# Layer 1's input projection by seven products of quarters instead of eight, with the sums of weights made by accumulating DMAs

## The chip, the cores and the metric

The kernel runs on one core of one Trainium2 chip. TensorE multiplies matrices, VectorE (DVE), ScalarE (ACT) and GpSimd (POOL) work on tiles of 128 partitions, and 16 DMA engines move data between HBM and SBUF; they are fed by the queues of SP, ScalarE and GpSimd, each of which issues in order. The metric is the time of one execution on the device in microseconds, the median of several runs.

## The reference

Two layers over 1024 tokens of 2048 channels. Layer 0 is an attention layer. Layer 1, to which the change belongs, is a pooling layer:

```python
h = _rmsnorm(x, pre_g) * (1 + scale) + shift            # 1024 x 2048
proj = h @ w_in                                         # w_in: 2048 x 4096
y = _multiscale_pool(proj[..., :POOL_WIDTH], pool_w, pool_scale) * jax.nn.silu(proj[..., POOL_WIDTH:])
x = x + gate * _rmsnorm(y @ w_out, post_g)
```

`_multiscale_pool` takes four groups of 512 channels, subtracts each value from the mean over 2, 4, 8 or 16 positions, and multiplies each group by a 512 x 512 matrix. The first 2048 columns of `w_in` give the values u, the other 2048 the gates.

## The kernel before

Everything is in float32. A product is made in three passes on TensorE (`PASSES`): each operand is split into a rounded part h and a rest l (`split`: ScalarE casts, VectorE subtracts), and hh, hl and lh are summed in PSUM. One pass of one k (128 rows) on one tile of 128 columns and 512 tokens is one matmul of 128x512.

Weights come by `w_tiles`: a raw tile `wr` of 512 KB (four k x 256 columns, two buffers) is loaded on SP's queue and split into tiles `wh` and `wl` of two k each (four buffers each). Before, one such pair serves two column tiles, two k and both halves of the tokens, 24 products.

The order of the stages is that of the code, and a scheduler settles the order on each engine when the kernel is built; what is pinned (`keep_in_program_order`) stays. The attention runs over 32 units (a group of four heads and 128 queries). In each, GpSimd multiplies the gate tile `zt` by the inverse sums `rs` (L857), which SP has sent through memory (`lsd`, `rs`), and VectorE multiplies the unit's output by it (`y`, L863); only then is the PSUM bank of the output free for the next unit. Then the output projection runs for the first half of the tokens (n = 0) and for the second (n = 1); its result is transposed (L1053), scaled and split into the operand tiles `hT`, 16 k for each half. While the last rows of n = 1 are normalised, `first_gates` computes the first six gate tiles of n = 0 (L1034, stored in `sd`). Layer 1's projection follows by groups: `project1` for four value tiles of both halves, `pooled` (the window sums, alternating between VectorE and GpSimd, L1097), `project1` for the gates, and the pooled products `mx`. The results `yt` (one buffer) are stored to `y1d` for the last output projection.

Of the kernel before, what the change touches and what calls it, by code (L numbers as in the profile page):

```python
# [17 lines left out]
P = 128  # L18
# [17 lines left out]
LEAD = 28  # L36
LAG = 2
# [8 lines left out]
BRIDGE = 6  # L46
# [30 lines left out]
def tile_backbone(ctx, tc, ins, out):  # L77
# [13 lines left out]
    def dram(shape, name):  # L91
        return tc.dram_tile(shape, F32, name=name)
# [46 lines left out]
    sd = [dram([P, HL], f"sd{m}") for m in range(BRIDGE)]  # L139
    y1d = [[dram([P, 4, 2, HL], f"y1d{g}_{n}") for n in range(NH)] for g in range(4)]  # L140

# [646 lines left out]
    with ExitStack() as st:  # L788
# [41 lines left out]
        GATE = nc.gpsimd  # L830

# [73 lines left out]
        for u, (g, n) in enumerate(units):  # L905
# [7 lines left out]
            for c in order(u):  # L913
# [5 lines left out]
                elif c == "P":  # L919
                    product()  # L920
                elif c == "N":
                    nxt = start(u + 2)
                    next(nxt, None)
                else:
                    weights = next(ahead, None) or weights
            if u in SUMS:
                mod_sums(SUMS.index(u))
# [14 lines left out]
    def out_proj(ev, w, y, gps, n, resid, finish, ahead=None, last=False):  # L942
# [15 lines left out]
        def gated(t, cg, ps, gp):  # L958
            o = ev.tile([P, 512], F32, tag="og", name="og", bufs=18)
# [48 lines left out]
    hT = [[None] * NH for _ in range(KC)]  # L1008
    with ExitStack() as st:
# [16 lines left out]
        def first_gates():  # L1026

            for m0 in range(0, BRIDGE, 2):
                outs = [psg.tile([P, HL], F32, tag="g", name="g") for _ in range(2)]
                for k0, nk, w in w_tiles(ins["od_w_in"][0][:, (16 + m0) * P : (18 + m0) * P], 2 * P):  # L1030
                    for m, o in enumerate(outs):
                        for k in range(k0, k0 + nk):
                            for i, (a, b) in enumerate(PASSES):
                                mm = nc.tensor.matmul(  # L1034
                                    o, lhsT=w[a][:, k - k0, m * P : (m + 1) * P], rhs=hT[k][0][:, b],
                                    start=(k == 0 and i == 0), stop=(k == KC - 1 and i == 2),
                                )
                                tc.keep_in_program_order(mm)
                        yield
                for m, g in enumerate(outs, m0):  # L1040
                    zt = ev.tile([P, HL], F32, tag="og", name="zt", bufs=18)
                    nc.scalar.activation(zt, g, AF.Silu)
                    store(sd[m], zt)

        for n in range(NH):
            og = out_proj(ev, ins["ev_w_out"][0], ys[n], gpd[0], n, lambda t: x[t * P : (t + 1) * P, :], add_norm, None if n else other_half(yd))
            gates = first_gates() if n else iter(())
            list(islice(gates, LEAD))
            for k in range(KC):
                list(islice(gates, 1))  # L1050
                t = pst.tile([P, HL], F32, tag="t", name="t")
                for tb in range(4):
                    tr = nc.tensor.transpose(t[:, tb * P : (tb + 1) * P], og[tb][k // 4][:, (k % 4) * P : (k % 4 + 1) * P], ident)  # L1053
                    if n:
                        tc.keep_in_program_order(tr)
                w = ev.tile([P, HL], F32, tag="nw", name="nw", bufs=2)
                nc.scalar.activation(w, t, AF.Identity, bias=b1[:, k : k + 1], scale=s1[:, k : k + 1])
                hT[k][n] = act_tile(k, n)
                split(hT[k][n][:, 0], hT[k][n][:, 1], w, "pool")
            list(gates)  # L1060


    w_in1 = ins["od_w_in"][0]
    with ExitStack() as st:
        ev = pool(st, "ev2")
# [104 lines left out]
```

## Time and profile before

| | |
|---|---|
| median of 3 runs | 3043.45 us (3042.88 to 3043.84) |
| the profiled execution | 3042.5 us, its span 3040.8 us |
| granted TensorE clock, mean | 0.989 |
| TensorE busy | 2951.6 us, 97% |
| VectorE, ScalarE, GpSimd busy | 1612.4, 1067.0, 169.3 us |
| DMA moved | 530.32 MB, mean 174 GB/s |

The span runs from the first to the last instruction; the rest of the execution's time lies around it. A share of 97% is a mean over stages; what a change in one stage is worth is read in its own windows.

### The profile page before, as it was taken

What the parts mean: (1) busy time and instruction counts of PE and PEld (TensorE: products, weight loads), DVE (VectorE), ACT (ScalarE), POOL (GpSimd) and SP (SyncE); (2) the same over time, 40 slices, a digit from 0 to 9 for tenths busy, and PEclk for the clock granted to TensorE, in tenths of its full rate; (3) what the DMA queues carried; (4) which work ended last, traced back from release to release, by engine and by line L of the source; (5) the groups of instructions that cost most, each with busy time, mean ns of one, the idle gap of its engine ahead of it and who ended that gap; (6) DMA issues with size and microseconds to landing.
All of it is one profiled execution on the core that took longest, in us unless ns stands there. A gap on an engine that the chain in (4) does not pass through costs nothing.

```text
span 3040.8 us, 38187 instructions
## 1 busy us (share of the span) xinstructions
PE 2951.6 (97%) x14038; PEld 2456.4 (81%) x14038; DVE 1612.4 (53%) x2866; ACT 1067.0 (35%) x2060; POOL 169.3 (6%) x150
## 2 busy tenths in 40 slices
PE   5999999999999999999899999999999999999998
PEld 4788888778887878888778888888888888888887
DVE  7979875663347478888633543533333323233434
ACT  5553322211212267766632443522222212122322
POOL 0000000000000000002200210300000002000000
PEclk8999999999999999999999999999999999999999
DMA  8858878886668554446554635414122121454634
GB/s 314 291 179 258 257 238 260 280 291 218 210 220 298 178 151 142 115 150 167 143 188 157 237 97 170 150 49 143 45 95 76 63 90 49 151 191 146 252 109 163
DMA packets 373009, 530.32 MB, mean 174 GB/s; under 512 B 28644, under 2 KB 215894, under 8 KB 371670
## 3 DMA queue, kind: packets, MB, share of 16 engines
q1 hardware_dynamic: 287990, 445.81, 45.5%
q10 hardware_dynamic: 84832, 82.07, 7.9%
q8 instruction: 110, 1.80, 0.2%
q14 instruction: 77, 0.63, 0.1%
HBM read 428.88 MB, written 98.91 MB: 174 GB/s over the span
## 4 chain that ended last, share of the span: by engine, by line
PE 80%; DMA 11%; DVE 5%; issue 2%; ACT 1%; POOL 0%; SPq 0%; ACTq 0%; DVEq 0%; POOLq 0%
PE g L184 41%; PE g L953 21%; DMA mraw<-in_od_mod_w_dram 5%; PE o L895 4%; PE mx L184 3%; PE s L252 3%; PE t L841 3%; DVE mac L345 2%; PE g L1034 2%; DMA mraw<-in_ev_mod_w_dram 2%; DMA lsd<-ls 1%; DMA rs<-lsd 1%; DMA wr<-in_od_w_out_dram 1%; PE c L258 1%; DMA zt<-in_ctx_dram 1%
## 5 line engine op out<-in xcount | busy, mean ns | idle before, releaser
L147 DVE TENSOR_TENSOR wl<-wr,wh 128x512 fp32r<-128x512 f32 (+1 forms) x576 | 395.8, 692 | 843.2 <-ACT wh L144 831.1
L144 ACT CAST wh<-wr 128x512 fp32r<-128x512 f32 (+1 forms) x576 | 350.5, 616 | 1152.3 <-PE g L184 584.3
L184 PE MATMUL g<-h,wh 128*128 128x512 f32 x2368 | 743.0, 394 | 1.9 <-ACT h L144 1.8
L953 PE MATMUL g<-wh,a 128*128 128x512 f32 x1920 | 593.7, 390 | 0.4 <-ACT wh L144 0.4
L184 PE MATMUL g<-a,wh 128*128 128x512 f32 x1856 | 571.2, 389 | 0.0
L184 PEld LDWEIGHTS g<-h,wh 128*128 128x128 f32 x2368 | 445.3, 190 | 93.6 <-ACT h L144 2.5
L184 PE MATMUL g<-h,wl 128*128 128x512 f32 x1184 | 465.0, 393 | 5.0 <-DVE wl L147 5.0
L953 PEld LDWEIGHTS g<-wh,a 128*128 128x128 f32 x1920 | 360.2, 188 | 75.1 <-ACT wh L144 0.8
L345 DVE SCALAR_TENSOR_TENSOR mac<-mraw,csil,mac 128x512 f32<-128x512 f32 x480 | 357.1, 748 | 112.6 <-DMA mraw<-in_od_mod_w_dram 61.1
L184 PEld LDWEIGHTS g<-a,wh 128*128 128x128 f32 x1856 | 348.4, 188 | 72.3
L953 PE MATMUL g<-wl,a 128*128 128x512 f32 x960 | 373.7, 389 | 0.0
L184 PE MATMUL g<-a,wl 128*128 128x512 f32 x928 | 360.7, 389 | 0.0
L184 PEld LDWEIGHTS g<-h,wl 128*128 128x128 f32 x1184 | 224.4, 190 | 53.0 <-DVE wl L147 6.5
L953 PEld LDWEIGHTS g<-wl,a 128*128 128x128 f32 x960 | 180.2, 188 | 37.5
L184 PEld LDWEIGHTS g<-a,wl 128*128 128x128 f32 x928 | 174.2, 188 | 36.3
L147 DVE TENSOR_TENSOR tl<-t,th 128x512 fp32r<-128x512 f32 x236 | 160.0, 685 | 39.2 <-ACT th L144 37.8
L144 ACT CAST th<-t 128x512 fp32r<-128x512 f32 x236 | 135.9, 585 | 111.3 <-PE t L841 110.3
L895 PE MATMUL o<-th,vt 128*128 128x512 f32 x472 | 156.2, 412 | 2.5 <-ACT th L144 2.5
L841 PE MATMUL t<-ident,p 128*128 128x128 f32 x944 | 138.9, 276 | 10.2 <-DVE tl L147 9.8
L841 PEld LDWEIGHTS t<-ident,p 128*128 128x128 f32 x944 | 114.4, 141 | 38.1 <-DVE tl L147 15.6
L857 POOL TENSOR_TENSOR zt<-zt,rs 128x512 f32<-128x512 f32 x32 | 49.6, 1552 | 1426.0 <-DMA zt<-zd 1075.5
L252 PE MATMUL s<-kt,qt 128*128 128x512 f32 x384 | 103.4, 404 | 0.0
(216 smaller groups left out, 3002.6 us busy)
## 6 DMA issues: line engine op xcount, KB each, us to landing
mraw<-in_ev_mod_w_dram SPq DMA_DIRECT2D x192, 256.0 KB, 4.2
mraw<-in_od_mod_w_dram SPq DMA_DIRECT2D x192, 256.0 KB, 4.2
wr<-in_od_w_in_dram SPq DMA_DIRECT2D x76, 512.0 KB, 3.7
wr<-in_ev_w_in_dram SPq DMA_DIRECT2D x68, 512.0 KB, 4.7
mraw<-in_ev_mod_w_dram SPq DMA_DIRECT2D x64, 512.0 KB, 4.7
wr<-in_ev_w_out_dram SPq DMA_DIRECT2D x64, 512.0 KB, 3.7
wr<-in_od_w_out_dram SPq DMA_DIRECT2D x64, 512.0 KB, 5.2
qd<-hl ACTq DMA_DIRECT2D x64, 256.0 KB, 3.9
```

The costliest lines, as they stand in the source:

```text
L144: nc.scalar.copy(dst_h, src)
L147: (lo or nc.vector).tensor_tensor(dst_l, src, f32(dst_h), op=ALU.subtract)
L184: pin(nc.tensor.matmul(o, lhsT=w[a][:, kk, m * P : (m + 1) * P], rhs=rhs(n, k, b), start=(k == 0 and i == 0), stop=(k == kc - 1 and i == 2),))
L252: pin(nc.tensor.matmul(s[:, sl], lhsT=qt[:, h, a], rhs=kt[:, b, sl], start=i == 0, stop=i == 2))
L258: pinned(nc.tensor.matmul(cs[:, hh], lhsT=qt[:, h + hh, a], rhs=kt[:, b, L:], start=i == 0, stop=i == 2))
L345: nc.vector.scalar_tensor_tensor(a, w, c, a, op0=ALU.mult, op1=ALU.add)
L841: pin(nc.tensor.transpose(t[:, h * P : (h + 1) * P], ps[h][:, i * P : (i + 1) * P], ident))
L857: GATE.tensor_tensor(zt, zt, rs.rearrange("p q h -> p h q"), op=ALU.mult)
L895: pin(nc.tensor.matmul(outs[u], lhsT=vt[:, a, kb], rhs=b, start=(i == 0 and jj == 0), stop=(last and jj == 2)))
L953: nc.tensor.matmul(o, lhsT=y[k][:, a, t * P : (t + 1) * P], rhs=wt[b][:, k - k0, :], start=(k == 0 and i == 0), stop=(k == KC - 1 and i == 2),
L1034: mm = nc.tensor.matmul(o, lhsT=w[a][:, k - k0, m * P : (m + 1) * P], rhs=hT[k][0][:, b], start=(k == 0 and i == 0), stop=(k == KC - 1 and ...
```

## The change

The token halves (index 1 or 2 of the operand) and the halves of the 2048 input channels (k 0 to 7 and 8 to 15) cut h into quarters x11, x12 (n = 0) and x21, x22 (n = 1). `quarter(a, b, q, c)` is the weights' part a (upper or lower half of the rows), b (values or gates), q (half of its eight k) and c (256 columns, eight of them). The projection is made of seven products of quarters, each with 16 column tiles, eight k and 512 tokens:

- products one and two, `first_products`: x11 by quarter (0,0), stored as `p1d`, and x12 by (1,0) on top of it, stored as `ud`, the values of n = 0. They are pinned around the transposes of n = 1 (28 steps of 12 products ahead, then two between transposes).
- products three and four, `second`: two sums of operands by sums of weights, less p1d, stored as `u2d` and `u3d`. The weights of product three are (0,1)+(0,0)+(1,1), kept in memory as `td`; of product four (1,1)+(0,1).
- products five, six and seven by groups: `values` (x22 by td+(1,0), with u3d and ud), then `gates` for n = 1 (weights (0,1)+(0,0)) and for n = 0 ((1,1)). The pooled products of a group are made after the values of the next (`mixes`, `mixed`).

Sums of weights are made by DMAs on GpSimd's queue that add what they bring to the tile in SBUF. For the first four c (`EARLY`) they are made in the attention, in tiles `qa` and `qb`, and stored to `td` and `te`. The other operands (x22, s4, s1) are stored to `opd` and reloaded into free operand tiles in three lots. The raw tiles have a ring of six in products three and four and of four afterwards; loads of intermediate tiles (`fetched`) share three buffers `pl`. The window sums of the pooling go to VectorE alone, the casts of h to ScalarE.

```diff
-BRIDGE = 6
+EARLY = 4
+BETWEEN = 2
+PL = 3
+RING = 6
+    w_in1 = ins["od_w_in"][0]
+    def quarter(a, b, q, c):
+        r = (8 * a + 4 * q) * P
+        return w_in1[r : r + 4 * P, b * D + c * 256 : b * D + (c + 1) * 256].rearrange("(k p) m -> p k m", p=P)
...
+        def early_sums(u):
+            c, q, step = u // 8, u // 4 % 2, u % 4
+            if c >= EARLY:
+                return
+            dma = nc.gpsimd.dma_start
+            if step == 0:
+                early[:] = [ap.tile([P, 4, 256], F32, tag=tag, name=tag, bufs=1) for tag in ("qa", "qb")]
+                for r, b in zip(early, (0, 1)):
+                    load(r, quarter(b, 1, q, c))
+            elif step == 1:
+                for r, b in zip(early, (0, 1)):
+                    dma(out=r, in_=quarter(0, b, q, c), accum_op=ALU.add)
+            elif step == 2:
+                load(te[q][c], early[1])
+                dma(out=early[0], in_=quarter(1, 1, q, c), accum_op=ALU.add)
+            else:
+                load(td[q][c], early[0])
...
+    def quarter_tiles(src):
+        for q in range(2):
...
+            load(r, first)
+            for o in others:
+                if o[0] == "store":
+                    store(o[1], r)
+                else:
+                    nc.gpsimd.dma_start(out=r, in_=o[1], accum_op=ALU.add)
+            for i in range(2):
...
+                split(h, l, raw[:, i * WT : (i + 1) * WT])
+                yield 4 * q + 2 * i, 2, [t.rearrange("p (k m) -> p k m", k=2) for t in (h, l)]
...
+    def sum_of(c, *quarters, kept=None, more=None):
+        def at(q):
+            r = [quarter(a, b, q, c) for a, b in quarters]
+            if more:
+                r.insert(0, more[q][c])
+            return [r[0], *(("add", o) for o in r[1:]), *([("store", kept[q][c])] if kept else [])]
+        return at
...
+        def first_products():
...
+            held = {}
+            for c in range(9):
+                if c < 8:
+                    held[c] = [psg.tile([P, HL], F32, tag="g", name="g") for _ in range(2)]
+                    yield from part(c, held[c], 0)
+                    evicted(c, held[c], p1d)
+                if c:
+                    outs = held.pop(c - 1)
+                    yield from part(c - 1, outs, 1)
+                    evicted(c - 1, outs, ud)
...
+        for k in range(8):
...
+            load(x11, xd[k])
+            load(x12, xd[k + 8])
...
+            x21, x22 = ws
...
+            nc.vector.tensor_tensor(s3, x21, x11, op=ALU.subtract)
+            nc.vector.tensor_tensor(x21, x21, x22, op=ALU.subtract)
+            nc.vector.tensor_tensor(x11, x11, x21, op=ALU.subtract)
+            nc.vector.tensor_tensor(x12, x12, x11, op=ALU.subtract)
+            for i, a in enumerate((x11, s3)):
+                ops[i][k] = acts[1, i].tile([P, 2, HL], F32R, tag="a", name="a")
+                operand(ops[i][k], a)
+            for i, a in enumerate((x22, x21, x12)):
+                store(opd[i][k], a)
...
+        def fetched(d, tag="pl", bufs=PL):
+            t = etile(tag, bufs)
+            load(t, d)
+            return t
...
+        def second(c, outs, accumulate):
+            if c < EARLY:
+                src = sum_of(c, more=(td, te)[accumulate])
+            else:
+                src = sum_of(c, (1, 1), (0, 1)) if accumulate else sum_of(c, (0, 1), (0, 0), (1, 1), kept=td)
+            product(outs, src, ops[accumulate], not accumulate)
+            for m, o in enumerate(outs, 2 * c):
+                p = ready.pop(0) if ready else fetched(p1d[m])
+                nc.vector.tensor_tensor(p, o, p, op=ALU.subtract)
+                store((u2d, u3d)[accumulate][m], p)
...
+            if c < 8:
+                held[c] = pair()
+                second(c, held[c], 0)
+            if c:
+                second(c - 1, held.pop(c - 1), 1)
+            if c == 3:
+                x22 = reloaded(0, 0, 0)
+            if c == 5:
+                s4t = reloaded(2, 0, 1)
...
+        def values(g, c2):
+            c, outs = 2 * g + c2, pair()
+            product(outs, sum_of(c, (1, 0), more=td), x22)
...
+        def gates(g, c2, outs, n):
+            c = 2 * g + c2
+            if n:
+                product(outs, sum_of(c, (0, 1), (0, 0)), s1t)
+            else:
+                product(outs, sum_of(c, (1, 1)), s4t, False)
+            for m, o in enumerate(outs, 2 * c):
+                p = fetched((u2d, u3d)[n][m])
...
         for g in range(4):
+            po = values(g, 0) + values(g, 1)
+            s1t = s1t or reloaded(1, 1, 0)
+            for f in mixes:
+                f()
+            held = [pair(), pair()]
+            for n in (1, 0):
+                for c2 in range(2):
+                    gates(g, c2, held[c2], n)
+            mixes = [lambda g=g, cc=cc, n=n, po=po: mixed(g, cc, n, po) for n in range(NH) for cc in (0, 2)]
```

GpSimd's queue in the attention, before, holds the 17 gate products of the first units one behind the other; this is the row as it stood.

```order
L857 TENSOR_TENSOR zt<-zt,rs 128x512 x17
L147 TENSOR_TENSOR yo<-y,yo 128x512
L857 TENSOR_TENSOR zt<-zt,rs 128x512
L147 TENSOR_TENSOR yo<-y,yo 128x512
L857 TENSOR_TENSOR zt<-zt,rs 128x512
```

In the changed kernel the same queue, from the gate product of unit 0 to that of unit 3, holds the first accumulating DMAs between them (the rows of L864 and L867; the numbers tell one buffer's contents from the next).

```order
L896 TENSOR_TENSOR zt_9340<-zt_9340,rs_9147 128x512
L864 DMA qa_9368<-in_od_w_in_dram 128x4x256
L864 DMA qb_9369<-in_od_w_in_dram 128x4x256
L867 DMA qa_9368<-in_od_w_in_dram 128x4x256
L864 DMA qb_10237<-in_od_w_in_dram 128x4x256
L896 TENSOR_TENSOR zt_9558<-zt_9558,rs_9377 128x512
L864 DMA qa_10236<-in_od_w_in_dram 128x4x256
L867 DMA qa_10236<-in_od_w_in_dram 128x4x256
L864 DMA qb_11112<-in_od_w_in_dram 128x4x256
L896 TENSOR_TENSOR zt_9775<-zt_9775,rs_9594 128x512
L864 DMA qa_11111<-in_od_w_in_dram 128x4x256
L867 DMA qa_11111<-in_od_w_in_dram 128x4x256
```

About one set of three sums stands ahead of each gate product, until all 24 are through ahead of that of unit 8. In layer 1 itself, the same queue held the pooling's window sums before, where the second, third and fourth group begin:

```order
L1097 TENSOR_TENSOR s_19257<-s_19255 128x541
L1097 TENSOR_TENSOR s_19265<-s_19263 128x541
L1097 TENSOR_TENSOR s_19276<-s_19274 128x541
L1097 TENSOR_TENSOR s_19284<-s_19282 128x541
L1097 TENSOR_TENSOR s_19531<-s_19529 128x541
```

Now it holds nothing but accumulating DMAs. These are those of products three and four for c = 5 to 7 (two sums on each tile of product three, one on each of product four).

```order
L1067 DMA wr2_20073<-in_od_w_in_dram 128x4x256
L1067 DMA wr2_20110<-in_od_w_in_dram 128x4x256
L1067 DMA wr2_20073<-in_od_w_in_dram 128x4x256
L1067 DMA wr_20155<-in_od_w_in_dram 128x4x256
L1067 DMA wr2_20110<-in_od_w_in_dram 128x4x256
L1067 DMA wr_20190<-in_od_w_in_dram 128x4x256
L1067 DMA wr2_20235<-in_od_w_in_dram 128x4x256
L1067 DMA wr2_20272<-in_od_w_in_dram 128x4x256
L1067 DMA wr2_20235<-in_od_w_in_dram 128x4x256
L1067 DMA wr2_20317<-in_od_w_in_dram 128x4x256
L1067 DMA wr2_20272<-in_od_w_in_dram 128x4x256
L1067 DMA wr2_20352<-in_od_w_in_dram 128x4x256
```

The second sum on a tile stands two places behind the first, which must have landed. On SP's queue the weight loads of the projection stood alone before, four to a `project1`:

```order
L160 DMA wr_20122<-in_od_w_in_dram 128x4x256
L160 DMA wr_20180<-in_od_w_in_dram 128x4x256
L160 DMA wr_20238<-in_od_w_in_dram 128x4x256
L160 DMA wr_20296<-in_od_w_in_dram 128x4x256
L160 DMA wr_20404<-in_od_w_in_dram 128x4x256
```

Now, at the same products three and four, loads of `p1d` and of the first lot stand among them.

```order
L1062 DMA wr2_20110<-in_od_w_in_dram 128x4x256
L1195 DMA pl_19705<-opd0_7_227 128x512
L1062 DMA wr_20155<-in_od_w_in_dram 128x4x256
L1195 DMA pl_19785<-p1d8_252 128x512
L1195 DMA pl_19789<-p1d9_253 128x512
L1195 DMA pl_19861<-p1d6_250 128x512
L1062 DMA wr_20190<-in_od_w_in_dram 128x4x256
L1062 DMA wr2_20235<-in_od_w_in_dram 128x4x256
L1195 DMA pl_19865<-p1d7_251 128x512
L1195 DMA pl_19945<-p1d10_254 128x512
L1062 DMA wr2_20272<-in_od_w_in_dram 128x4x256
```

A load into `pl` waits for that buffer to come free, and the weight loads behind it wait with it.

## Rows read from the trace of the kernel before

**Rows 1.** The page's first part: busy us, share of the span, instructions.

```profile
PE 2951.6 (97%) x14038; PEld 2456.4 (81%) x14038; DVE 1612.4 (53%) x2866; ACT 1067.0 (35%) x2060; POOL 169.3 (6%) x150
```

**Rows 2.** Windows by stage: attention's units 0 to 8, n = 1, first gates, layer 1.

```profile
core 0: us, PE busy (x) PEld busy (x) DVE busy (x) ACT busy (x) POOL busy (x), PEclk, DMA share, GB/s
1076.00:1235.00 159.00, 157.40 (x898) 129.54 (x897) 130.94 (x225) 111.92 (x229) 12.87 (x9) 1.00 0.48 145
1707.00:1888.00 181.00, 181.00 (x831) 150.18 (x830) 85.36 (x168) 73.69 (x153) 32.23 (x32) 1.00 0.45 146
1888.00:1963.00 75.00, 75.00 (x364) 62.25 (x363) 49.59 (x115) 47.33 (x95) 28.26 (x32) 1.00 0.48 155
1963.00:2682.00 719.00, 719.00 (x3162) 593.34 (x3161) 225.23 (x350) 160.05 (x266) 38.32 (x34) 1.00 0.27 88
```

**Rows 3.** The chain that ended last, in order of time: start us, us, what.

```profile
1888.50 39.44 PE g L1034 x174
1927.94 0.44 PE t L1053 x4
1928.38 1.38 PE g L1034 x6
...
1962.72 107.21 PE g L184 x473
2069.94 11.19 PE mx L184 x48
```

**Rows 4.** Waits, 1960 to 2680 us: us in total, times, longest us.

```profile
ACT wh L144 <- PE g L184: 321.0, 104, 8.9
ACT yt L144 <- DMA y1d<-yt: 60.3, 22, 5.6
...
SPq L160 <- DVE wl L147: 613.4, 69, 11.1
```

**Rows 5.** Groups by form, 1530 to 2680 us: the projection's products.

```profile
L184 PE MATMUL g<-a,wh 128*128 128x512 f32 x1856 | 571.2, 389 | 0.0
L184 PE MATMUL g<-a,wl 128*128 128x512 f32 x928 | 360.7, 389 | 0.0
...
L1034 PE MATMUL g<-a,wh 128*128 128x512 f32 x192 | 60.7, 397 | 0.0
...
L1034 PE MATMUL g<-a,wl 128*128 128x512 f32 x96 | 37.5, 390 | 0.0
```

**Rows 6.** Groups by form, 1963 to 2682 us: splits and pooling; mean ns.

```profile
L147 DVE TENSOR_TENSOR wl<-wr,wh 128x512 fp32r<-128x512 f32 x144 | 102.6, 713 | 330.7 <-ACT wh L144 320.8 <-DMA a<-y1d 8.8
L144 ACT CAST wh<-wr 128x512 fp32r<-128x512 f32 x145 | 90.3, 623 | 342.2 <-PE g L184 321.0 <-DVE wl L147 13.2 <-PE mx L184 7.1
...
L1097 POOL TENSOR_TENSOR s<-s 128x541 f32<-128x541 f32 x24 | 26.5, 1105 | 579.7 <-DVE s L1097 554.0 <-DVE po L147 25.7
...
L1097 DVE TENSOR_TENSOR s<-u 128x543 f32<-128x543 f32 x32 | 23.1, 721 | 40.1 <-ACT u L1087 39.4
L147 DVE TENSOR_TENSOR po<-s,po 128x512 fp32r<-128x512 f32 x32 | 22.1, 690 | 14.2 <-ACT po L144 13.6
L1104 DVE SCALAR_TENSOR_TENSOR s<-s,u 128x512 f32<-128x512 f32 x32 | 22.1, 690 | 0.8
...
L1097 POOL TENSOR_TENSOR s<-s 128x529 f32<-128x529 f32 x8 | 11.6, 1455 | 7.6 <-DVE s L1097 7.6
...
L1102 DVE TENSOR_TENSOR s<-s,edge 128x8 f32<-128x8 f32 x32 | 5.2, 164 | 12.2 <-POOL s L1097 11.8
```

**Rows 7.** Windows by DMA: 2 KB rows, weight tiles alone, 4 KB rows.

```profile
600.00:620.00 20.00, 20.00 (x90) 16.57 (x89) 12.83 (x19) 4.88 (x11) 0.00 (x0) 1.00 0.94 296
1980.00:2000.00 20.00, 20.00 (x90) 16.56 (x89) 2.83 (x5) 3.67 (x6) 0.00 (x0) 1.00 0.17 53
2820.00:2840.00 20.00, 20.00 (x90) 16.57 (x89) 5.25 (x8) 4.16 (x8) 0.00 (x0) 1.00 1.03 406
```

**Rows 8.** Timeline of GpSimd and VectorE: gate products 1, 5 and 9; y.

```profile
1075.99 1.55 POOL L857 TENSOR_TENSOR zt<-zt,rs 128x512 f32<-128x512 f32 x1 [1075.55 <-DMA zt<-zd]
...
1156.66 1.56 POOL L857 TENSOR_TENSOR zt<-zt,rs 128x512 f32<-128x512 f32 x1 [17.19 <-DVE l L262]
...
1166.94 0.68 DVE L863 TENSOR_TENSOR y<-o,zt 128x512 f32<-128x512 f32 x1
...
1234.55 1.55 POOL L857 TENSOR_TENSOR zt<-zt,rs 128x512 f32<-128x512 f32 x1 [19.26 <-DMA ma<-md]
```

**Rows 9.** DMA issues: tile, queue, count, KB each, median us to landing.

```profile
wr<-in_od_w_in_dram SPq DMA_DIRECT2D x76, 512.0 KB, 3.7
...
y1d<-yt ACTq DMA_DIRECT2D x32, 512.0 KB, 2.6
```

More of the change, by code (lines that the diff above doesn't have):

```diff
@@ L36 @@
 LEAD = 28
+OG = 16
+EARLY = 4
+BETWEEN = 2
+PL = 3
+RING = 6
 LAG = 2
@@ L1045, in tile_backbone @@
[L1045 to L1060, printed above, removed]
@@ L1063, in tile_backbone, with part, evicted @@
-    w_in1 = ins["od_w_in"][0]
-    with ExitStack() as st:
+        def first_products():
+            def part(c, outs, i):
+                for k0, nk, w in quarter_tiles(sum_of(c, (i, 0))):
+                    products(outs, [(k0, nk, w)], lambda k: hT[8 * i + k][0], i == 0, tc.keep_in_program_order)
+                    yield
+            def evicted(c, outs, d):
+                for m, o in enumerate(outs):
+                    t = ev.tile([P, HL], F32, tag="pe", name="pe", bufs=2)
+                    nc.scalar.copy(t, o)
+                    store(d[2 * c + m], t)
+            held = {}
[8 more added lines that the diff above has]
+                    evicted(c - 1, outs, ud)
@@ new lines, in operand @@
+        def operand(o, w):
+            split(o[:, 0], o[:, 1], w)
+        og = out_proj(ev, ins["ev_w_out"][0], ys[0], gpd[0], 0, lambda t: x[t * P : (t + 1) * P, :], add_norm, other_half(yd))
+        for k in range(KC):
+            w = columns_of(0, k, og)
+            store(xd[k], w)
+            hT[k][0] = act_tile(k, 0)
+            operand(hT[k][0], w)
+        og = out_proj(ev, ins["ev_w_out"][0], ys[1], gpd[0], 1, lambda t: x[t * P : (t + 1) * P, :], add_norm)
+        early = first_products()
@@ new lines, in tile_backbone, with etile, pair, product @@
+        list(early)
+    with ExitStack() as st:
+        s_two = st.enter_context(ExitStack())
+        ev = pool(s_two, "ev2a")
+        raw_tiles.append(lambda: ev.tile([P, 1024], F32, tag="wr2", name="wr2", bufs=RING - 2))
+        raws_made[0], ring[0] = 0, RING
+        def etile(tag, bufs):
+            return ev.tile([P, HL], F32, tag=tag, name=tag, bufs=bufs)
+        def fetched(d, tag="pl", bufs=PL):
+            t = etile(tag, bufs)
+            load(t, d)
+            return t
+        def pair():
+            return [psg.tile([P, HL], F32, tag="g", name="g") for _ in range(2)]
+        def product(outs, src, op, first=True):
+            for group in twos(quarter_tiles(src)):
+                products(outs, group, lambda k: op[k], first)
+        ready = [fetched(p1d[m]) for m in range(2)]
+        def second(c, outs, accumulate):
[8 more added lines that the diff above has]
+                store((u2d, u3d)[accumulate][m], p)
+        def reloaded(i, n, half):
+            r = []
+            for k in range(8):
+                t = acts[n, half].tile([P, 2, HL], F32R, tag="a", name="a")
+                w = fetched(opd[i][k])
+                split(t[:, 0], t[:, 1], w)
+                r.append(t)
+            return r
+        held = {}
+        for c in range(9):
+            if c < 8:
[7 more added lines that the diff above has]
+                s4t = reloaded(2, 0, 1)
+        s_two.close()
```

154 lines of the change are left out of this document (93 added, 61 removed).

## The prediction

> **What bounds the kernel now.** I read the busy line of the page first: TensorE is busy 97% of the span, VectorE 53%, ScalarE 35%, GpSimd 6% [rows 1]. The windows by stage then say where the other 3% lie: from 1888 us to 2682 us, the whole of layer 1's input projection, TensorE is busy in every microsecond at a granted clock of 1.00 (2.4 GHz), while the DMA share is 0.48 and then 0.27 [rows 2]. The chain in order of time shows the same from the other side: nothing but products of L1034 and L184 and the products of the pooled groups, one behind the other, with four transposes of 0.44 us each time between the first ones [rows 3]. 473 products in 107.21 us are 0.2267 us each; the 0.39 us that the lines show is one product from start to end, and they overlap. So this stage is worth its number of products times 0.2267 us, as long as nothing else becomes late: ScalarE's casts of weights wait for TensorE to free a buffer, not the reverse, and SP's queue waits for VectorE in the same way [rows 4].
>
> **What is removed.** The projection has 3072 products of 128x512 (1856 + 928 + 192 + 96 in [rows 5]). Seven quarters of 16 column tiles x 8 k x 3 passes are 2688. 384 x 0.2267 = **87.1 us less** on an engine that never waits there. Transposes and the pooled products stay as many as they were.
>
> **What is added on the engines.** Weight tiles serve half as many products, so there are 96 more casts on ScalarE (0.623 us) and 96 more differences on VectorE (0.713 us) [rows 6], one pair for 12 products (2.72 us of TensorE). The 32 steps of the pooling on GpSimd (1.1 to 1.5 us) go to VectorE (0.72 us) [rows 6]. Where VectorE has most to do is the last group, with four steps per half tile: 32 differences of weights 22.8, pooling 8 x (4 x 0.72 + 0.16 + 0.69 + 0.69) = 35.4, 20 sums and products of 128x512 at some 0.72 = 14.4 and 8 differences of yt 5.5, 78 us in the 87 us of TensorE's 384 products. It fits, at 0.9, and I count nothing for it (the fourth rival does). The 32 casts of h that leave GpSimd for ScalarE lie half beside the output projection of n = 1 and half beside the pinned products, where ScalarE was busy 74 of 181 us and 47 of 75 us [rows 2].
>
> **What is added on the DMA engines** decides. Prices, as time of all 16 engines: a window with nothing but weight tiles of 512 KB (rows of 1 KB) has share 0.17 at 53 GB/s, so one tile of 0.524 MB costs 1.68 us. A window of tiles with rows of 2 KB, 0.94 at 296 GB/s, gives 0.83 us for 256 KB. One of 512 KB tiles with 4 KB rows, 1.03 at 406 GB/s, gives 1.33 us (td, te, y1d) [rows 7]. An **accumulating DMA** is nowhere in the trace. It brings in a weight tile, so it is at least 1.68 us; it also has to read the tile that it adds to, and if that takes as long again it is 3.36 us. I take 2.35 us: a weight tile plus the reading half of a 1.33 us move, the nearest row for a tile that leaves SBUF. Every sum below has these three values in this order.
>
> The Trainium skill ("Collectives: The Full Stack", section "The bandwidth ceiling: the fold count and why AG ≠ RS ≠ AR") says that a sum in the DMA path costs two source reads on the same reading side and so half the rate; by it the upper price would hold and the kernel would come out slower, which is the third rival. No row of before shows it.
>
> 1. *The second half of products three and four (c = 4 to 7, 87.1 us of TensorE).* 16 loads 26.9, 24 sums 40.3 / 56.4 / 80.6, 8 stores of td 10.6, 40 moves of 256 KB (p1d, u2d and u3d, the second lot) 33.2: 111 / 127 / 151 us. Six raw tiles of 5.44 us (24 products each) let this start 32.7 us ahead, inside the first half, which uses 16 x 1.33 + 40 x 0.83 = 54.5 of its 87.1 us and so leaves 0.37 x 32.7 = 12 us. Lost on TensorE: **12 / 28 / 52 us**.
> 2. *Products five to seven and the pooled products, 87.1 us of TensorE for each group.* 4 td 5.3, 8 sums 13.4 / 18.8 / 26.9, 8 loads 13.4, 4 pool weights 6.7, 32 moves of 256 KB 26.6, 8 stores of y1d 10.6: 76 / 81 / 89.5 us. It is uneven: the four pooled products take 23.9 us in 21.8, the quarter that is not summed 13.3 in 21.8, and only four raw tiles are ahead. I take 3 us a group for the middle price and 6 us once for the third lot: **5 / 18 / 48 us** (the upper end is what the three full parts lack, 10.5 us a group).
> 3. *The early sums in the attention (c = 0 to 3).* The order puts all 24 between the gate products zt of units 0 and 8 on GpSimd's queue, and the stores of td and te before lsd and rs on SP's, both served in order; zt 1 to 9 stand at 1076 to 1235 us [rows 8]. 16 loads, 24 sums and 16 stores are 89 / 105 / 129 us; these 159 us have share 0.48 [rows 2], so 82 us are free. A late zt holds y on VectorE and with it the bank for the next unit, but zt ends 8.7 us before y begins (1158.2 to 1166.9) [rows 8]. What is over, less that: **0 / 14 / 38 us**.
>
> What I cost at nothing: the p1d and ud products lie under 182 us of TensorE with 127 us of DMA, and the chain of subtractions and splits behind each transposed pair (4 x 0.7 + 2 x 1.3, under 6 us) lies under the 10.9 us of products pinned between pairs. On SP's queue the loads of p1d, which wait for one of three pl buffers, stand among the weight loads; the tile behind pl_19865 (wr2_20272) is due five products after that buffer comes free, so this costs nothing either. The ScalarE queue already waits 60.3 us for the one yt buffer's stores [rows 4]. With a store landing in 2.6 us [rows 9] eight yt take some 32 us of a group's 87; they hold TensorE only if weights are cast behind them with less than 10.9 us of cast tiles left, so they are part of the fourth rival.
>
> **Sum.** The profiled execution took 3042.5 us (span 3040.8), 0.95 us under the median. 3042.5 - 87.1 + 60 = 3015.4 with the middle price (28 + 18 + 14); 3042.5 - 87.1 + 17 = 2972.4 with the lower; 3042.5 - 87.1 + 138 = 3093.4 with the upper. With the 0.95 us: 2973, 3016 and 3094. The middle one counts every loss as if it stood on TensorE's path; the early sums need not (they may trail behind unit 8 where there is DMA time), so I put the likeliest time at **3010 us**, 33 us under the median.
>
> **Rivals.**
> - *The sums are priced at the middle*, 3010 us, range 2990 to 3035: chance 0.42. For it: reading and writing of one transfer overlap in the rows above, and only the additional read is new.
> - *The sums cost what a load costs*, and the DMA engines keep up: 2973 us. For it: the engines stand idle three quarters of this stage now [rows 2]. Against it: 111 us of work in 87. Chance 0.24.
> - *The sums cost two reads*, and the stage is bound by DMA: 3094 us, slower. It becomes slower than before where the losses reach 87.1 us: between 2.35 us (60 lost) and 3.36 us (138), that is at about 2.7 us for one sum. Chance 0.24.
> - *An engine's queue in order is the new wait*: yt or a late product in front of weight casts, VectorE in the last group at 0.9. Two stalls of 8.8 us (pooling one tile pair) a group in four groups, 4 x 2 x 8.8 = 70 us at most, half of it likely: 3010 + 25 = 3035 us, on either side. Chance 0.10.
>
> 0.2% of 3043 us, 6 us, is about what this kernel's measurement can tell. Faster by more: 0.24 + 0.37 + 0.02 + 0.03 = 0.66; within: 0.07; slower: 0.27. The 8-in-10 range takes in the lower price and reaches into the upper one: 2965 to 3078 us.
>
> **What would show it right or wrong.** TensorE's count falls by 384 and its idle time, now none between 1888 and 2682 us, shows what the sums cost: waits of wh on DMA wr. The DMA share should be near 1 in the second half of products three and four and 0.9 in the groups; if it stays under 0.8 and TensorE waits all the same, latency of a queue is the cause and not the rate. The engine time of one sum can be read from windows with sums. In the attention, zt should not end later than y needs it; if units 0 to 8 grow, the third term is right. The prediction is wrong if one sum costs more than 2.7 us or the issue on GpSimd is itself slow (more than some 3.6 us each, 24 in 87 us), or if the casts are held by yt.

## The result and the profile after

The changed kernel takes **3127.11 us** (median of 4 runs, 3125.22 to 3128.79) against 3043.16 us (3042.41 to 3043.84, 4 runs): ratio 1.0276, 95% interval 1.0258 to 1.0294. It is slower, where 3010 us was forecast.

The busy line and the software queue of the page of the kernel after (packets, MB, share of 16 engines):

```profile
PE 2908.4 (93%) x13654; PEld 2409.0 (77%) x13654; DVE 1765.1 (57%) x3126; ACT 1140.2 (37%) x2202; POOL 208.8 (7%) x164
...
q0 software_dynamic: 42240, 41.95, 8.7%
```

TensorE is busy 93% of the span instead of 97% [rows 1]. Its products of the projection, in the groups by line, are 1792 + 896 = 2688 where [rows 5] had 3072, exactly the 384 less that were counted:

```profile
L1089 PE MATMUL g<-a,wh 128*128 128x512 f32 x1792 | 570.3, 402 | 63.0 <-ACT wh L163 51.8 <-DVE pl L1216 9.5 <-ACT a L163 1.6
...
L1089 PE MATMUL g<-a,wl 128*128 128x512 f32 x896 | 355.4, 399 | 2.2 <-DVE wl L166 2.1
```

Only the accumulating DMAs use the software queue: 0.087 x 3123.4 us / 80 = **3.40 us of all 16 engines for one sum**, which no row of before could show. The price is the time that the packets took, and other traffic might have stretched it. There is no sign of that: the packets of the larger hardware queue took no longer beside the sums (first line, 0.519 x 3123.4 = 1621 us for 528.14 MB) than in e2_no_sums, a run below that issues none of them (second line, 0.550 x 2990.0 = 1645 us).

```profile
q1 hardware_dynamic: 333014, 528.14, 51.9%
```

```profile
q1 hardware_dynamic: 333014, 528.14, 55.0%
```

Windows of the kernel after: attention's units 0 to 8 by the clock of before, then first products, products 3 and 4 in two parts, groups (us, then PE, PEld, DVE, ACT, POOL busy, granted clock, DMA share, GB/s):

```profile
1076.00:1235.00 159.00, 128.52 (x681) 105.55 (x680) 100.31 (x171) 87.03 (x176) 32.52 (x24) 0.91 0.98 246
1950.00:2131.00 181.00, 181.00 (x832) 150.03 (x831) 97.91 (x186) 90.00 (x173) 17.78 (x16) 1.00 0.67 215
2131.00:2216.00 85.00, 79.31 (x339) 64.79 (x338) 26.48 (x40) 16.87 (x28) 6.42 (x5) 0.96 0.81 238
2216.00:2353.00 137.00, 107.55 (x433) 85.03 (x431) 43.68 (x67) 29.12 (x52) 26.96 (x21) 0.91 1.02 252
2353.00:2759.00 406.00, 369.00 (x1537) 298.72 (x1537) 253.35 (x423) 133.77 (x230) 38.32 (x30) 0.94 0.91 261
```

Against [rows 2], the DMA share goes from 0.48 to 0.98 in units 0 to 8 of the attention and from 0.27 to between 0.81 and 1.02 in products 3 to 7. In the first products (0.67) TensorE stays busy in every microsecond; in the others it stands idle and runs at a granted clock under 1.00.

Where the time went is read from the first product of each stage:

| stage | nominal or before, us | after, us | lost | forecast, lower / taken / upper |
|---|---|---|---|---|
| attention, first product of outputs to first output projection | 460.1 | 520.1 | 60 | 0 / 14 / 38 |
| first output projection and first products (355.7 + 768 x 0.2267 + 16 x 0.44) | 536.8 | 537.1 | 0 | 0 |
| products 3 and 4 (768 x 0.2267) | 174.1 | 222.0 | 48 | 12 / 28 / 52 |
| groups and last projection (1536 x 0.2267 + 358.9) | 707.1 | 770.3 | 63 | 5 / 18 / 48 |

171 us lost, 87.1 removed: 84, and the spans differ by 82.6 us. Before the change TensorE was busy 157.4 of 159 us in units 0 to 8 and in every microsecond of layer 1's projection [rows 2]. The waits of the kernel after (us in total, times, longest), first TensorE's over the whole span:

```profile
PE g L1089 <- ACT wh L163: 51.8, 11, 15.4
PE o L934 <- DVE ls L304: 48.7, 7, 16.5
...
PE g L1089 <- DVE pl L1216: 9.5, 1, 9.5
```

TensorE waits for cast weights in layer 1 and for ls in the attention. VectorE's, GpSimd's and SP's waits in 1076 to 1330 us say why ls is late: y, ahead of it on VectorE, waits for zt, and GpSimd and SP stand behind landings of qa, qb and rs:

```profile
DVE y L902 <- POOL zt L896: 50.2, 8, 16.7
...
POOL qa L867 <- DMA qa<-in_od_w_in_dram: 53.5, 8, 9.8
POOL zt L896 <- DMA rs<-lsd: 31.0, 3, 14.4
...
SPq L869 <- DMA qa<-in_od_w_in_dram: 46.1, 7, 14.7
SPq L866 <- DMA qb<-in_od_w_in_dram: 42.9, 8, 12.9
```

GpSimd's timeline shows one such place, a zt that stood 14.42 us for rs, and two sums right behind it, ahead of the next zt:

```profile
1170.13 1.51 POOL L896 TENSOR_TENSOR zt<-zt,rs 128x512 f32<-128x512 f32 x1 [14.42 <-DMA rs<-lsd]
1173.38 1.30 POOL L864 DMA_DIRECT2D qa<-in_od_w_in_dram  x1 [1.74 <-DMA qa<-in_od_w_in_dram]
1174.76 1.29 POOL L864 DMA_DIRECT2D qb<-in_od_w_in_dram  x1
```

In layer 1, the chain in order of time (start us, us, what) is no longer products but landings of weights:

```profile
2253.47 10.18 DMA wr<-in_od_w_in_dram
2264.11 0.63 ACT wh L163
...
2266.08 12.49 DMA wr<-in_od_w_in_dram
...
2279.13 12.94 DMA wr<-in_od_w_in_dram
2292.36 16.36 DMA wr<-in_od_w_in_dram
```

DMA issues after (tile, queue, count, KB, median us to landing): a load lands in 5.7 us and a store of y1d in 5.8, where [rows 9] had 3.7 and 2.6, and a sum, which follows its load, takes another 10.1 us:

```profile
wr<-in_od_w_in_dram SPq DMA_DIRECT2D x80, 512.0 KB, 5.7
wr<-in_od_w_in_dram POOLq DMA_DIRECT2D x56, 512.0 KB, 10.1
y1d<-yt ACTq DMA_DIRECT2D x32, 512.0 KB, 5.8
```

### The profile page after: what moved, and what is told of

It reads as the page before. It is cut to its first block, busy times and chain, and to the rows that moved or that the text cites. A ratio compares the mean times of both kernels' runs of the same rounds, so it can differ in the third digit from the quotient of the medians.

```text
span 3123.4 us, 38876 instructions
## 1 busy us (share of the span) xinstructions
PE 2908.4 (93%) x13654; PEld 2409.0 (77%) x13654; DVE 1765.1 (57%) x3126; ACT 1140.2 (37%) x2202; POOL 208.8 (7%) x164
## 3 DMA queue, kind: packets, MB, share of 16 engines
q1 hardware_dynamic: 333014, 528.14, 51.9%
q0 software_dynamic: 42240, 41.95, 8.7%
## 4 chain that ended last, share of the span: by engine, by line
PE 37%; DMA 15%; DVE 3%; issue 2%; ACT 1%; POOL 1%; SPq 0%; ACTq 0%; DVEq 0%; POOLq 0%
PE g L993 21%; PE g L1089 11%; DMA wr<-in_od_w_in_dram 5%; PE o L934 2%; PE t L880 1%; DMA y1d<-yt 1%; DMA lsd<-ls 1%; DMA pl<-opd 1%; DMA wr<-in_od_pool_w_dram 1%; PE s L271 1%; DMA rs<-lsd 1%; DMA wr<-in_od_w_out_dram 1%; DVE wl L166 1%; PE t L1140 0%; DMA wr<-td 0%
## 5 line engine op out<-in xcount | busy, mean ns | idle before, releaser
L166 DVE TENSOR_TENSOR wl<-wr,wh 128x512 fp32r<-128x512 f32 (+1 forms) x664 | 448.7, 683 | 719.1 <-ACT wh L163 690.4
L163 ACT CAST wh<-wr 128x512 fp32r<-128x512 f32 (+1 forms) x664 | 399.7, 615 | 1099.9 <-PE g L993 279.5
L934 PE MATMUL o<-th,vt 128*128 128x512 f32 x472 | 162.8, 427 | 51.3 <-DVE ls L304 48.7
L934 PEld LDWEIGHTS o<-th,vt 128*128 128x128 f32 x472 | 81.1, 198 | 63.4 <-issue 49.9
## 6 DMA issues: line engine op xcount, KB each, us to landing
wr<-in_od_w_in_dram POOLq DMA_DIRECT2D x56, 512.0 KB, 10.1
```

Source lines behind the costliest of these rows:

```text
L163: nc.scalar.copy(dst_h, src)
L166: (lo or nc.vector).tensor_tensor(dst_l, src, f32(dst_h), op=ALU.subtract)
L934: pin(nc.tensor.matmul(outs[u], lhsT=vt[:, a, kb], rhs=b, start=(i == 0 and jj == 0), stop=(last and jj == 2)))
```

## The experiments

**Theories.** One: a sum costs two reads and the DMA engines are the bound wherever sums are issued. Two: the landings, waited for in order by SP, GpSimd and the ring of raw tiles, are the loss, whatever they cost the engines. Each stage is measured as in the table above:

| run | attention | products 3, 4 | groups + last | time, us |
|---|---|---|---|---|
| kernel after | 520.1 | 222.0 | 770.3 | 3127.11 |
| e1_plain | 495.2 | 191.6 | 750.8 | 3059.07 |
| e2_no_sums | 470.9 | 178.8 | 721.6 | 2991.75 |
| e3_early0 | 458.6 | 278.0 | 776.0 | 3129.29 |
| e4_early_plain | 488.1 | 223.1 | 773.5 | 3098.59 |
| e5_swap | 521.7 | 224.6 | 772.2 | 3132.60 |
| e6_pin | 483.2 | 224.6 | 771.4 | 3095.31 |
| e7_pin_engine | 483.3 | 186.6 | 772.6 | 3061.15 |
| e8_engine | 518.3 | 191.6 | 774.5 | 3099.83 |
| e9_two | 460.6 | 213.3 | 769.0 | 3058.26 |
| e10_packed | 467.6 | 182.2 | 766.6 | 3032.63 |
| e11_queue | 457.4 | 215.4 | 756.0 | 3042.64 |
| e12_both | 468.7 | 179.6 | 759.8 | 3020.59 |
| e13_quarter | 525.2 | 219.9 | 745.8 | 3108.93 |

e1 to e5, e8 and e13 are single runs; the work ahead of the attention, the same in all, ended between 1071 and 1082 us, so a total of one run is good to some 10 us. The stages are good to less: the kernel after, e5, e8 and e13 have the same attention, and it took 518.3 to 525.2 us. The ratios and intervals at the end of this section are against the kernel before as timed beside each run (medians 3044.17 to 3047.07 us).

**Sums as plain DMAs, and none.**

```
-                    nc.gpsimd.dma_start(out=r, in_=o[1], accum_op=ALU.add)
+                    nc.gpsimd.dma_start(out=r, in_=o[1])      # e1, at all three places; e2: left out
```

> All 80 accumulating DMAs become plain ones of the same size, queue, order and destination; left out is the adding, so the weights of products 3 to 7 are not sums. Theory 1 (rate: a sum takes two reads, 3.40 us of all 16 engines by the page of the kernel after, and the DMA engines bind where sums are issued): each falls to about 1.7 us, the time goes to about 2973 us (2960 to 3000), with the first out_proj starting at 1533 to 1545 us for 1594. Theory 2 (order: GpSimd's and SP's queues stand behind landings of 7 to 10 us, whatever the transfers cost the engines): waits of GpSimd and SP stay, at least 90 of the 172 us lost stay, the time is 3045 to 3127 us.

> The 80 accumulating DMAs are not issued at all; left out is the adding of weights, each tile holds its first quarter alone. What is left is the removed products, the casts, the round trips of p1, u2, u3, u and the reloads. Theories 1 and 2 both: 2945 to 2975 us, near 3043 - 87 = 2956. Theory 3 (a queue of ScalarE or VectorE, or the small round trips, are the loss): above 3000 us.

Page and windows of e1 (attention up to 1330 us, products 3 and 4, groups), then windows of e2 (the whole attention, then the same two):

```profile
q0 software_dynamic: 11520, 41.95, 4.2%
```

```profile
1082.00:1330.00 248.00, 222.83 (x1209) 183.19 (x1208) 179.35 (x307) 151.47 (x308) 35.28 (x35) 0.94 0.77 238
2115.00:2306.00 191.00, 179.43 (x769) 145.51 (x767) 70.53 (x107) 46.17 (x79) 19.52 (x26) 0.98 0.84 286
2306.00:2693.00 387.00, 361.55 (x1534) 293.85 (x1535) 252.40 (x422) 133.81 (x230) 22.47 (x30) 0.96 0.81 274
```

```profile
1082.00:1553.00 471.00, 442.81 (x2578) 372.45 (x2578) 366.37 (x741) 317.58 (x698) 68.81 (x47) 0.99 0.60 176
2090.00:2268.00 178.00, 175.35 (x766) 142.77 (x765) 72.56 (x111) 48.04 (x81) 0.00 (x0) 1.00 0.72 237
2268.00:2627.00 359.00, 352.14 (x1540) 289.26 (x1539) 250.35 (x420) 133.98 (x227) 0.00 (x0) 1.00 0.75 249
```

A plain DMA of the same bytes costs 0.042 x 3057.3 / 80 = 1.61 us of 16 engines, so the adding costs 1.79 us each. Taking that away gives back 68 us of the 171, and taking the DMAs away 67 us more. Theory one failed as a total, by 59 us over its range; e1 is inside theory two's range (3045 to 3127), although the price that theory two leaves out gave back 68 us. e2, at 2991.75 us, misses the 2945 to 2975 of both by 17: some 30 us are lost without any sum. By stage the theories part: products 3 and 4 lose 48, 17.5 and 5 us in the three runs, which follows the engines' time; the attention loses 60, 35 and 11, the groups with the last projection 63, 44 and 14.5, where the price is less than half of it.

**No early sums, and early sums plain.**

```
-EARLY = 4
+EARLY = 0                                                     # e3
-                    dma(out=r, in_=quarter(0, b, q, c), accum_op=ALU.add)
+                    dma(out=r, in_=quarter(0, b, q, c))       # e4, and the one below it
```

> No sums during the attention; products 3 and 4 of columns 0 to 3 form theirs as columns 4 to 7 do. Both theories: the first out_proj starts near 1533 us for 1594, 61 us given back. Theory 1: columns 0 to 3 then cost what columns 4 to 7 did, 49 us, so 3105 to 3125 us in all. Theory 2: less than half of the 61 us is lost again, because the ring's six slots let the loads run ahead: 3066 to 3095 us.

> Only the 24 DMAs issued during the attention are plain in place of accumulating; left out is the adding in these 24, so products 3 and 4 of columns 0 to 3, and the values, have other weights. Theory 1: the first out_proj starts at 1533 to 1545 us, the time is 3066 to 3080 us. Theory 2: the waits of GpSimd on landings stay, zt comes as late as before, the first out_proj starts at 1580 us or later, the time is 3110 to 3127 us.

Windows of e3, attention and the first columns of products 3 and 4:

```profile
1076.00:1330.00 254.00, 252.43 (x1438) 208.24 (x1437) 211.65 (x365) 179.62 (x369) 20.93 (x14) 1.00 0.46 135
2073.00:2206.00 133.00, 86.94 (x336) 68.50 (x336) 26.67 (x40) 17.65 (x31) 33.53 (x26) 0.82 1.10 258
```

Without early sums the attention loses nothing (458.6 us), and products 3 and 4 lose 56 us more: moved, not saved, at a DMA share of 1.10; the total, 3129.29 us, is 4 over theory one's range. In layer 1's products 3 and 4 the rate decides. e4 gives back 32 of 60 us in the attention, half way between the two theories, and its 3098.59 us stand between both ranges.

**Larger rows.**

```
-                r.insert(0, more[q][c])
+                r.append(more[q][c])
```

> In the 16 sums of the values the two operands change places: the quarter of the weights is loaded (rows of 1 KB) and the kept sum is added (rows of 4 KB); the output is the same sum. If a sum costs 3.40 us because it reads two sources (theory 1), the 80 sums keep about 272 us of 16 engines and the time is that of the kernel after, 3127 us (3118 to 3137). Rival: what costs is the number of packets (528 for a sum, 144 for the same bytes loaded plainly in the run with plain DMAs); then the 16 come to about 1.7 us each, the 80 sums to about 244 us, and 5 to 15 us come off the groups.

The software queue on its page:

```profile
q0 software_dynamic: 36096, 41.95, 8.4%
```

(0.084 x 3130.8 - 64 x 3.40) / 16 = 2.8 us for a sum with rows of 4 KB. Loads of such rows cost 1.33 us [rows 7], so the factor is still 2.1; the packets' size makes 0.6 of the 3.40 us. The time did not fall, and is inside the range expected of two reads. The rival is refuted as the main cause: the packets show it as well, since (36096 - 64 x 528) / 16 = 144 for a sum with rows of 4 KB is the count of a plain DMA in e1, and the sum still takes 2.8 us for its 1.61.

**The bunching.** The program has a step of the early sums in each of 32 units; the scheduler had moved them all ahead of the zt of unit 8. e9 and e10 keep the pins of e6; their products 3 and 4 add on GpSimd, as e7's below, with a ring of ten raw tiles for six.

```
-                    load(r, quarter(b, 1, q, c))
+                    pin(load(r, quarter(b, 1, q, c)))         # e6: pin around all seven DMAs
```

> The DMAs of the early sums keep the place in which the program has them, one step of four in each unit of the attention, over all 32 units, where the kernel after has all 24 between the zt of units 0 to 8. Nothing else changes. If the bunching is what costs 61 us in the attention (waits of SP and GpSimd on landings ahead of rs and zt, at a DMA share of 0.95), the first out_proj starts at 1533 to 1545 us and the time is 3066 to 3080 us. Rival: each sum between two zt holds GpSimd and SP wherever it stands; then 40 us or more of the 61 stay, 3105 to 3127 us.

> EARLY is 2, the early sums pinned: 12 sums, all in units 0 to 15 of the attention; products 3 and 4 add on GpSimd (ring of 10 slots), the groups keep their accumulating DMAs. In the run with all 24 pinned, units 0 to 15 lost nothing and units 16 to 31 lost 29 us. If the loss in the attention is a matter of the unit's length against the landings, the first out_proj starts at 1531 to 1543 us; products 3 and 4 then have 24 + 12 sums on GpSimd at 27 us per 24 in place of 56: about 190 us; groups 406. Sum 3061 - 29 + 6 = 3038 us (3025 to 3050). Rival: the sums cost the attention as many us each wherever they stand (29 us for 24): 3047 to 3060 us.

> As the one before with EARLY 4: all 24 early sums pinned in units 0 to 15, a step each half unit (two units of 19 us for four steps, where the kernel after has it in little more than one). DMA engines: 8 items of 16.2 us in 300 us at a share of 0.46 before, 0.89 in all. If the rate alone decides, nothing is lost in the attention and the time is about 3032 us. If the landings (7 to 9 us against half a unit of 9.5) hold SP's and GpSimd's queues, 15 to 40 us are lost there: 3047 to 3072 us.

```
-EARLY = 4
+EARLY = 2                                                     # e9
-            for c in order(u):
+            for at, c in enumerate(parts):                    # e10, parts = order(u)
+                if at == len(parts) // 2:
+                    early_sums(2 * u)
-            early_sums(u)
+            early_sums(2 * u + 1)
```

Windows of units 0 to 15 and 16 to 31, first of the kernel before (not among the rows ahead of the prediction), then of e6 and of e10:

```profile
1073.00:1386.00 313.00, 308.19 (x1766) 255.75 (x1765) 260.08 (x463) 219.33 (x455) 27.73 (x18) 0.99 0.48 142
1386.00:1533.00 147.00, 132.35 (x814) 115.09 (x813) 105.10 (x278) 98.36 (x244) 41.27 (x29) 0.98 0.53 146
```

```profile
1077.00:1391.00 314.00, 308.37 (x1764) 255.94 (x1764) 260.13 (x464) 219.14 (x455) 43.05 (x30) 0.99 0.70 191
1391.00:1560.00 169.00, 137.41 (x815) 118.59 (x814) 104.30 (x278) 98.93 (x244) 56.41 (x41) 0.93 0.79 203
```

```profile
1079.00:1399.00 320.00, 309.70 (x1766) 256.44 (x1765) 259.46 (x463) 219.82 (x456) 58.66 (x42) 0.99 0.89 234
1399.00:1547.00 148.00, 131.30 (x817) 114.23 (x816) 104.10 (x278) 97.78 (x244) 41.20 (x29) 0.99 0.51 141
```

Pinned at full price, the sums cost units 0 to 15 (19 us each) nothing: 314 us, where before has 313. Units 16 to 31 are some 9 us long (147 us for 16), and the same steps cost 22 us there: e6 got 37 of 60 us back, not 61 (3095 us, 15 over the forecast). e9, with 12 sums and none after unit 15, lost nothing in the attention, as expected; its 3058 us miss the range by 8 because the sums of columns 2 and 3 cost products 3 and 4 31 us more than in e10 (213.3 against 182.2), not 6. e10, all 24 in units 0 to 15 at a step each half unit, lost 7.5 us in the attention at a share of 0.89, where nothing was expected, and met its 3032 us: the same 24 sums at the same price cost 60 us bunched and 7.5 us paced.

**Adding on an engine.**

```
-                    nc.gpsimd.dma_start(out=r, in_=o[1], accum_op=ALU.add)
+                    other = raw_tiles[i > 1]()                # the next slot of the ring
+                    load(other.rearrange("p (k m) -> p k m", k=4), o[1])
+                    nc.gpsimd.tensor_tensor(raw, raw, other, op=ALU.add)
```

> As the one before, and in layer 1 the 56 sums are no accumulating DMAs: the second and third operand are loaded plainly into another slot of the ring and GpSimd adds them (2 to 3 us for 128x1024 by its 1.5 us for 128x512 in the attention). If layer 1 loses by the rate of the DMA engines, 22 us of products 3 and 4 and 19 us of the groups come back as in the run with plain DMAs, and the time is about 3026 us (3010 to 3045), under the kernel before. Rival: the ring's slots, now used up two or three times as fast, or GpSimd's adds become the wait: 3060 us or more.

> The sums of layer 1 on GpSimd as in the run before, the early sums bunched as in the kernel after. Rate: 3127 - 41 = 3086 us (3070 to 3105), with products 3 and 4 in about 192 us (222 now) and the groups in about 387 us (406 now). Rival, the ring's slots or GpSimd hold the products: 3120 us or more.

e7 has e6's pins, e8 has not. Products 3 and 4 fall to 187 and 192 us (nominal 174.1): the rate, confirmed there. The groups with the last projection do not fall at all (772.6 and 774.5, 770.3 in the kernel after). In e7's groups (2289 to 2695 us) ScalarE waits 64.4 us for GpSimd's sums and GpSimd, busy 77 of 406 us, waits 213.3 us for the loads that they need: the loads come late, the adds are not slow. e7 took 3061.15 us, 16 over the top of its range and inside its rival's: the groups' 19 us did not come, and the attention gave 37 us, not 61. e8's 3099.83 us are inside the range of the rate, by products 3 and 4 alone.

**What holds the groups.**

```
+                    part = 1 if ring[0] == 4 else 4           # e13, the groups' ring has 4 slots
-                    nc.gpsimd.dma_start(out=r, in_=o[1], accum_op=ALU.add)
+                    nc.gpsimd.dma_start(out=r[:, :part], in_=o[1][:, :part], accum_op=ALU.add)
-            load(t, d)
+            fetch[0](t, d)                                    # e11: GpSimd's queue in the groups, adds on VectorE
```

> As with EARLY 2, and in the groups VectorE adds the second operand from a further ring slot, and the reloads of u, u2, u3 and of the gates are issued by GpSimd, so that SP's queue holds weights alone and stands behind no store of a gate (81 us in 27 waits in the kernel after). If the groups lose by the second read and by SP's order, they fall to 360 to 380 us and the time to 2995 to 3015 us. Rival: four ring slots, two for each tile, leave 11 us of products for a landing of 5 to 6 us and an add, so the slots are the wait, groups 400 us or more, 3030 us or more.

> The kernel after, with the 32 accumulating DMAs of the groups cut to a quarter of their bytes (128 KB each); left out is the adding for three quarters of the rows of those weights. Number, place, queue and waits of the DMAs stay. The groups took 405.7 us with whole sums and 358.6 without any. If the bytes are what costs 47 us (rate), a quarter of it stays: 365 to 375 us, the time about 3090 us. Rival: a second landing in each tile's chain, ahead of the casts in a ring of four slots, costs the same at a quarter of the bytes: the groups stay at 385 to 400 us, the time at 3107 us or more.

Windows of the groups of e13, then of e11:

```profile
2361.00:2741.00 380.00, 356.92 (x1537) 290.33 (x1537) 253.08 (x423) 134.58 (x229) 26.41 (x31) 0.98 0.78 247
```

```profile
2283.00:2681.00 398.00, 366.90 (x1542) 295.90 (x1541) 284.30 (x452) 133.69 (x228) 44.48 (x83) 0.96 0.81 266
```

With a quarter of the bytes the groups take 379.5 us, between the two expectations; the time, 3108.93 us, is in the rival's range only because the stages ahead of the groups were 8 us later than in the kernel after. Above e2's 358.6 us, whole sums cost 47.1 us and quarter sums 20.9: 26.2 us for three quarters of the bytes, so, if the cost is linear in them, 35 us that go with the DMA engines' time and 12 us that 32 further DMAs cost whatever their bytes. Checked on e1: 35 x 1.61 / 3.40 + 12 = 28.6 us; measured 387.1 - 358.6 = 28.5. All three are single runs, and the split is good to a few us. That the 12 us are the landing ahead of the cast, and whether the 35 us are the rate or longer landings, is argued and not shown. e11's groups took 397.2 us, not 360 to 380, and the last projection 358.9 (364.6 in the kernel after): 14 us together; its 3042.64 us are in the rival's range. Its VectorE still waits 58.9 us for loads of wr in 23 waits, and SP, ahead of the loads of the second operand, 63.8 us in 23 waits for the wl that frees the slot. So the four slots, two for each tile, fit as the cause; a larger ring was not tried, and it is not shown.

**Both remedies.** e10's early sums and products 3 and 4, e11's groups.

> The packed early sums of the run with EARLY 4 and the groups of the run with VectorE's adds and the reloads issued by GpSimd. The two edits touch different stages: the groups and the last out_proj together took 766.6 us with accumulating DMAs and 756.1 with VectorE's adds, so 3032 - 10 = 3022 us (3012 to 3030). Rival: the larger use of the ring by products 3 and 4 on GpSimd and the groups' loads disturb each other at the border, 3030 us or more.

3020.59 us (3005.75 to 3033.63, 6 runs), inside its range, ratio 0.9913, interval 0.989 to 0.9935: this version is 0.9% faster than the kernel before. e10 alone: 0.9951 (0.993 to 0.9972); e11: 0.999 (0.9979 to 1.0002); e9: 1.0038 (1.0025 to 1.0052); e7: 1.0047 (1.0029 to 1.0065); e6: 1.0168 (1.0151 to 1.0185).

## Why the prediction was wrong

- **384 products less, 87.1 us.** Right: the count fell by 384, the first products ran without a gap, and e2, without sums, came to 2991.75 us, 51 us under the kernel before.
- **The price of a sum, 2.35 us between 1.68 and 3.36: this step failed.** A sum costs 3.40 us, above the 2.7 us named as the point from which the kernel is slower; a plain DMA in its place costs 1.61. The argument for the middle was that reading and writing overlap and only the reading of a tile in SBUF is new. No row shows either: the 1.33 us, half of which it took for a tile that leaves SBUF, come from a window in which SP's queue only loads (x1d, y1d and weights). This step is worth 68 us of the time (e1). The Trainium skill ("Collectives: The Full Stack", section "The bandwidth ceiling: the fold count and why AG ≠ RS ≠ AR") states two source reads and half the rate for the reduce step of a ring collective. The sums here, 3.40 against 1.61 us, agree with it; with as many packets it is 2.8 against 1.61.
- **Transfers cost only what exceeds the free DMA time: this step failed too, in two of the three terms that rest on it.** e1 has the lower column's price, and lost 17.5 + 44 + 35 = 97 us where that column has 12 + 5 + 0 = 17. At the upper price the same working is 33 us short. The next three points tell where.
- **Products 3 and 4, 28 us.** Measured 48, inside the upper column's 52. Here the working was right and the price in it was not: plain DMAs leave 17.5 us against the lower column's 12.
- **Groups, 18 us.** Measured 63, above the upper 48. The price accounts for the step from 18 to 48, but not for e1, which lost 44 us where the lower column has 5. By the split above, the 63 us are 35 that go with the sums' DMA time, though the demand of a group fits into its 87.1 us at e1's price, 12 for a second DMA in each tile's chain, and 14.5 that e2 loses without any sum, 4 of them in the last projection; 1.6 more are lost there. What causes the 14.5 is open.
- **Early sums, 14 us.** Measured 60, above the upper 38. That they stand between the zt of units 0 to 8 was read from the order and is what happened. The term set their DMA time against the free DMA time, less the slack of zt. But SP waits for a sum's landing before the next rs and GpSimd for the one before it, and with 16 loads and 16 stores and no sum at all (e2) 11 us are lost, where 48 us of transfers in 82 free ones should cost nothing. At the right price the term would have been 38; the other 22 us are put down to these waits and not split further. That the place of the sums makes the loss is shown by e10: 7.5 us at the same price.
- **A further cost that no term had: the clock.** In 2131 to 2759 us after, 2309 products take 555.9 us of busy time, in e2 2306 take 527.5, at granted clocks of 0.91 to 0.96 (means between the two levels, 1.2 and 2.4 GHz, of stretches in which TensorE had stood idle) against 1.00 (2.4 GHz throughout). So some 28 us of the layer's 111 lost are slower products, not idle time. In the attention it is some 12 of the 60: 452.5 us of busy time in 1074 to 1594 us against 308.2 + 132.4 = 440.5 before.
- **The rivals.** "Two reads" is nearest to what happened: a price of 3.36 us forecast and 3.40 measured, 3094 us forecast and 3127 measured, and its chance was 0.24. "What a load costs" was not 2973 either: e1, which has just that price, took 3059. The in-order queue came true on SP and GpSimd in the attention, not where it was put: ScalarE waits 31.6 us for yt's stores in the groups (60.3 before [rows 4]), and TensorE waited only 2.1 us for VectorE's wl in them. Half of that rival's 70 us is 35, not the 25 that it added. The issue on GpSimd is 1.3 us, well under the 3.6 us named. The signs named for a bound by the rate came true: shares of 1.02 in products 3 and 4 and 0.91 in the groups, units 0 to 8 longer, wh late behind wr.
- **The sum.** The upper column (138) missed 171 by 33: 22 in the attention, 15 in the groups, -4 in products 3 and 4. The range, 2965 to 3078 us, was too low at its top: it ended 16 us under the upper column's own 3094, and its three terms were moved together by one price and had no bound for waits.

## What to carry to other kernels

Price a new kind of transfer by its nearest row on the side that hurts, and count two things for it: its time on the DMA engines and the landing that it adds to a chain through a short ring. Free DMA time is a bound on what fits and not a promise that nothing waits: plain DMAs cost 97 us where 17 did not fit. Look where the scheduler puts transfers that it may move: here the same 24 sums cost 60 us bunched and 7.5 us paced one step each half unit. A second load and an add on an idle engine in place of a sum gave back 30 us or more in products 3 and 4 and nothing in the groups; that the slots of the ring make the difference fits the waits and is not shown.

## What the runs showed of the hardware

- An accumulating DMA of 512 KB: 3.40 us of 16 engines, in 528 packets (42240 / 80), with rows of 1 KB; 2.8 us in 144 packets with rows of 4 KB; a plain one from the same queue 1.61 us in 144 packets (11520 / 80), though its source has rows of 1 KB too.
- Its landing takes 10.1 us in layer 1 (median), and its issue on GpSimd 1.3 us.
- At DMA shares of 0.70 (e6's units 0 to 15) and 0.89 (e10's) TensorE lost 1 and 7 us in 313; at 0.98 and 1.02 it stood idle a fifth of the stretch (30 of 159 us, 29 of 137). The share alone does not tell: e6's units 16 to 31, at 0.79, lost 22 us of 169. Nor does the mean over the span, 222 GB/s in the kernel after.
- Lost time costs twice: e3's first columns, idle 46 of 133 us, ran at a granted clock of 0.82, and their 336 products took 86.9 us of busy time instead of 76.2.
